# First loads of a linear attention kernel: three of four fp32 loads on SP's queue become casting loads on GpSimd's

## The chip, the core and the metric

The kernel runs on one core of a Trainium2 chip. A core has a matrix engine (TensorE, PE in the profile, with its weight loads as PEld), a vector engine (VectorE, DVE), a scalar engine (ScalarE, ACT), a general engine (GpSimd, POOL) and an engine that mostly issues transfers (SyncE, SP). The five run by themselves and meet at semaphores. Transfers between main memory (HBM) and the on-chip memory are issued by an engine and carried out by 16 DMA engines that all queues share. The metric is the device time of one execution in microseconds; 126.58 us is the median of three runs before the change (126.56 to 126.68).

## The reference

Linear attention with a ReLU feature map, over 96 heads (8 x 12), a sequence of 512 and a head size of 64, all in fp32:

```
Q_feat = np.maximum(0, Q)
K_feat = np.maximum(0, K)
KV = np.einsum('bhkd,bhkv->bhdv', K_feat, V)
K_sum = np.sum(K_feat, axis=2)
numerator = np.einsum('bhqd,bhdv->bhqv', Q_feat, KV)
denominator = np.einsum('bhqd,bhd->bhq', Q_feat, K_sum)
out = numerator / (denominator[:, :, :, None] + 1e-10)
```

Each of Q, K, V and the output is 12.58 MB. So 37.75 MB are read and 12.58 MB written, and each byte moves once.

## The kernel before

**Tiles.** The heads are cut into 24 groups of four for K and V, and into 12 steps of eight for Q and the output; a step `o` needs the groups `2o` and `2o + 1`. K or V of a group is one transfer that reads 0.5 MB in fp32, Q of a step one that reads 1 MB, the output of a step one store of 1 MB. Each lies as 128 rows (partitions), 4 KB of fp32 per row for K and V, 8 KB for Q and the output.

**Loads.** They are all written ahead of the compute. K and V of groups 0 and 1 come by SP (lines 103 to 107): four plain fp32 loads into two tiles `kv_first`, which take turns in the pool of the output tiles. Everything else comes by GpSimd (lines 92 to 100), in loads that cast to bf16 on the way, so that they write half of what they read: first Q of step 0 (line 108), then for each later step K and V of both groups and Q (lines 110 to 113). Behind the first Q, GpSimd makes the identity matrix (line 109, in two instructions). K tiles and V tiles have rings of 12 buffers, Q tiles 7. GpSimd's program is this list and nothing else.

**Compute.** For a group, `prep` (lines 136 and 138) makes on VectorE two masked ReLU copies of K (`kf`) and a masked copy of V (`vo`), and `prep_v` the other copy of V on ScalarE or VectorE (lines 143, 145). `mm_kv` (line 150) multiplies them into K-transposed times V, with the key sums beside it; `evac_kv` (line 160) copies that out of the accumulator. For a step, `qt` transposes Q on TensorE against the identity (line 171) and applies the ReLU (lines 177, 179); `denom` (lines 221 to 233) gives the reciprocal of the denominator; `out_t` (lines 201, 203) the numerator, transposed; `backs` transposes it back (line 239), multiplies by the reciprocal (line 245) and calls `store`. The last two steps are written out in finer pieces, with `out_u` in place of `out_t` for the last (lines 214, 216), and a few matmuls without a use (`idle`, line 188).

**Order.** The order of every engine's instructions is the order of the program text; semaphores are set from the data. Before the loop stand the preparation of groups 0 and 1, an fp32 copy of the identity by VectorE (line 270), the zeroing of buffers, the products of groups 0 and 1 and the transposes of Q of step 0.

**Stores.** A store by SP is held back. `store(o)` first issues a read of a few bytes from the K tile of the step that is five further on, into `scratch` (line 253), so that SP waits until that load has landed:

```
if o + DELAY < NO:
    nc.sync.dma_start(out=scratch, in_=k_sb[2 * (o + DELAY)][0:1, 0, :])
```

The first seven stores are held so; the rest follow as soon as they are computed (lines 258 and 260), and the last is issued in two halves.

Of the kernel before, what the change touches and what calls it, by code (L numbers as in the profile page):

```python
# [10 lines left out]
def kernel(  # L11
# [7 lines left out]
    nc = tc.nc  # L19
    B, H, S, D = Q.shape  # L20
    assert D == 64
    P = 128
# [4 lines left out]
    R = S * 4 // P  # L27
# [4 lines left out]
    NO = NG // 2  # L32
    assert NO * 8 == NH and R == 16 and RQ == 32
    DELAY = 5
    F32 = 2

    fp32 = mybir.dt.float32
    bf16 = mybir.dt.bfloat16
# [3 lines left out]
    def pool(name, bufs, **kw):  # L42
        return ctx.enter_context(tc.tile_pool(name=name, bufs=bufs, **kw))
# [7 lines left out]
    outp = pool("outp", DELAY + 2)  # L51
# [6 lines left out]
    def view(X, f):  # L58
        return X.rearrange("b h s d -> (b h s d)").rearrange("(n p f) -> n p f", p=P, f=f)

    Qr, Kr, Vr, Or = view(Q, RQ * D), view(K, R * D), view(V, R * D), view(out, RQ * D)
# [27 lines left out]

    q_sb, k_sb, v_sb = {}, {}, {}  # L90

    def load_kv(g):
        k_sb[g] = kin.tile([P, R, D], bf16, name="k_sb")
        nc.gpsimd.dma_start(out=k_sb[g].rearrange("p r d -> p (r d)"), in_=Kr[g], single_packet=True)  # L94
        v_sb[g] = vin.tile([P, R, D], bf16, name="v_sb")
        nc.gpsimd.dma_start(out=v_sb[g].rearrange("p r d -> p (r d)"), in_=Vr[g], single_packet=True)  # L96

    def load_q(o):
        q_sb[o] = qin.tile([P, U, 2 * D], bf16, name="q_sb")
        nc.gpsimd.dma_start(out=q_sb[o].rearrange("p u f -> p (u f)"), in_=Qr[o], single_packet=True)  # L100


    for g in range(F32):
        kv = outp.tile([P, 2, R, D], fp32, name="kv_first", tag="o_sb")
        k_sb[g], v_sb[g] = kv[:, 0], kv[:, 1]
        nc.sync.dma_start(out=k_sb[g].rearrange("p r d -> p (r d)"), in_=Kr[g])
        nc.sync.dma_start(out=v_sb[g].rearrange("p r d -> p (r d)"), in_=Vr[g])
    load_q(0)
    make_identity(nc, ident)
    for o in range(1, NO):  # L110
        load_kv(2 * o)
        load_kv(2 * o + 1)
        load_q(o)

    def zero(i):
# [146 lines left out]
    def out_tile():  # L262
        return outp.tile([P, RQ, D], fp32, name="o_sb", tag="o_sb")
# [50 lines left out]
    o = NO - 2  # L314
    g = 2 * NO - 2
# [9 lines left out]
    o_sb = out_tile()  # L325
# [42 lines left out]
```

## Time and profile before

| | |
|---|---|
| median of three runs | 126.58 us |
| the profiled execution | 126.52 us |
| its span, first to last instruction | 124.7 us |
| mean granted clock of TensorE | 0.95 |
| busy: PE, DVE, ACT, POOL | 86.0, 81.1, 79.3, 33.1 us |
| moved per second over the span, reads and writes of HBM | 403 GB/s |
| loads by SP before: K0, V0, K1, V1 | 4 of 512 KB written each |
| loads by GpSimd: K and V | 22 + 22 of 256 KB written each |
| loads by GpSimd: Q | 12 of 512 KB written each |

The profile is of one execution. Its times are in microseconds from the first instruction. A line of the timeline has a start, a duration, an engine, a line of the kernel and what was written from what; the bracket at its end is the idle time before it and what ended that. `SPq` is SP's issuing of a transfer, and L106 is line 106. Bandwidth in slices and windows is of bytes written, so a casting load shows half of what it reads. K0 stands for K of group 0, V1 for V of group 1, Q0 for Q of step 0, and so on.

### The profile page before, as it was taken

The page shows a single profiled execution, that of the slowest core. Times are in us where ns is not written, and L with a number is a line of the kernel's source. Part 1 is how long each engine was busy: PE and PEld are TensorE (multiplying, and loading weights), DVE is VectorE, ACT ScalarE, POOL GpSimd, SP SyncE. Part 2 cuts the span into 40 slices and gives each one's busy share as a digit, 9 for nine tenths or more (in the row PEclk, how much of TensorE's full clock was granted, in tenths as well). Part 3 has the DMA queues.
Part 4 walks back from the last instruction along what each step waited for, and adds up shares of the span by engine and source line. Part 5 has one row for each costly group of instructions (what it writes and reads, how often), then busy time and mean ns, then how long its engine had stood idle before and what let it go on. Part 6 is the DMA issues. An engine that isn't in the chain of part 4 may idle for free.

```text
span 124.7 us, 2672 instructions
## 1 busy us (share of the span) xinstructions
PE 86.0 (69%) x1075; PEld 78.5 (63%) x1075; DVE 81.1 (65%) x176; ACT 79.3 (64%) x114; POOL 33.1 (27%) x62
## 2 busy tenths in 40 slices
PE   0041196998989899894598599399777587797600
PEld 0040194997878788793597499299576486696500
DVE  2605743949798897979247845935928918979600
ACT  0251549989898997989249558666839646837100
POOL 6924433415253341142133124034022000000000
PEclk9999999999999999999769959958999999999996
DMA  3999999999999999999999999999999999999993
GB/s 133 322 285 277 216 205 210 213 210 215 207 213 208 210 214 327 257 215 300 282 215 282 302 213 258 324 213 234 342 223 218 322 257 215 319 416 420 426 416 143
DMA packets 10748, 32.68 MB, mean 262 GB/s; under 512 B 1392, under 2 KB 1392, under 8 KB 9328
## 3 DMA queue, kind: packets, MB, share of 16 engines
q0 software_dynamic: 8064, 17.83, 74.7%
q1 hardware_dynamic: 2672, 14.68, 29.2%
q8 instruction: 8, 0.13, 0.4%
q14 instruction: 4, 0.03, 0.1%
HBM read 37.75 MB, written 12.58 MB: 403 GB/s over the span
## 4 chain that ended last, share of the span: by engine, by line
DMA 34%; DVE 26%; PE 25%; ACT 5%; issue 2%; SPq 1%; DVEq 1%; ACTq 0%; POOLq 0%
DMA v_sb<-in_V_dram 14%; DVE o_sb L245 13%; DMA q_sb<-in_Q_dram 13%; PE ps_kv L150 11%; DMA kv_first<-in_V_dram 8%; PE ps_bk L239 6%; PE ps_qt L171 4%; DVE kf L136 3%; ACT qt L179 3%; DVE vo L138 3%; ACT kvd L160 2%; PE ps_ot L201 2%; DVE vo L145 2%; DVE den L229 1%; DVE rec L233 1%
## 5 line engine op out<-in xcount | busy, mean ns | idle before, releaser
L150 PE MATMUL ps_kv<-vo,kf 128*128 128x132 bf16 x384 | 31.3, 247 | 18.4 <-ACT vo L143 7.9
L150 PEld LDWEIGHTS <-kf 128*128 128x128 bf16 x384 | 28.9, 111 | 19.7 <-DVE vo L138 10.3
L245 DVE TENSOR_TENSOR o_sb<-ps_bk,rec 128x1024 f32<-128x1024 f32 x24 | 28.4, 1220 | 16.7 <-PE ps_bk L239 16.7
L160 ACT CAST kvd<-ps_kv 64x260 bf16<-64x260 f32 (+1 forms) x54 | 18.7, 346 | 19.0 <-PE ps_kv L150 16.8
L179 ACT ACTIVATE qt<-ps_qt 128x1024 bf16<-128x1024 bf16 x23 | 22.4, 1027 | 4.9 <-PE ps_qt L171 4.8
L203 ACT COPY ot_sb<-ps_ot 128x1024 f32<-128x1024 f32 x22 | 21.9, 1014 | 2.1 <-PE ps_ot L201 1.3
L239 PE MATMUL ps_bk<-ident,ot_sb 128*128 128x128 f32 x192 | 23.0, 273 | 0.0
L136 DVE TENSOR_SCALAR kf<-k_sb,mask 128x1024 bf16<-128x1024 bf16 x44 | 18.3, 457 | 5.8 <-DMA k_sb<-in_K_dram 5.8
L94 POOL DMA_DIRECT2D k_sb<-in_K_dram x22 | 12.7, 578 | 34.1 <-DMA q_sb<-in_Q_dram 16.8
L239 PEld LDWEIGHTS ps_bk<-ident,ot_sb 128*128 128x128 f32 x192 | 20.8, 141 | 0.0
L171 PE MATMUL ps_qt<-ident,q_sb 128*128 128x128 bf16 x192 | 15.3, 243 | 5.6 <-DMA q_sb<-in_Q_dram 5.6
L96 POOL DMA_DIRECT2D v_sb<-in_V_dram x22 | 13.1, 597 | 19.7 <-DMA k_sb<-in_K_dram 12.0
L171 PEld LDWEIGHTS <-q_sb 128*128 128x128 bf16 x192 | 13.7, 110 | 6.6 <-DMA q_sb<-in_Q_dram 6.4
L201 PE MATMUL ps_ot<-qt,kvd 128*128 128x256 bf16 x88 | 13.5, 284 | 4.0 <-DVE o_sb L245 4.0
L201 PEld LDWEIGHTS <-kvd 128*128 128x128 bf16 x88 | 8.5, 101 | 6.5 <-issue 5.4
L138 DVE TENSOR_SCALAR vo<-v_sb,mask 128x1024 bf16<-128x1024 bf16 x22 | 10.8, 489 | 1.6 <-DMA v_sb<-in_V_dram 1.6
L143 ACT ACTIVATE vo<-v_sb,mask 128x1024 bf16<-128x1024 bf16 x10 | 11.5, 1154 | 0.2
L221 PEld LDWEIGHTS <-qt 128*128 128x128 bf16 x192 | 6.7, 97 | 4.7 <-ACT qt L179 3.4
L221 PE MATMUL ps_den<-kvd,qt 128*128 128x16 bf16 x192 | 7.5, 179 | 2.6 <-ACT qt L179 2.1
L100 POOL DMA_DIRECT2D q_sb<-in_Q_dram x12 | 6.7, 558 | 8.0 <-DMA v_sb<-in_V_dram 5.0
L224 DVE SCALAR_TENSOR_TENSOR own<-ps_den,mask_h 128x256 f32<-128x256 f32 x12 | 5.0, 417 | 3.3 <-PE ps_den L221 3.3
L145 DVE TENSOR_SCALAR vo<-v_sb,mask 128x1024 bf16<-128x1024 bf16 x12 | 5.8, 484 | 0.0
(27 smaller groups left out, 29.5 us busy)
## 6 DMA issues: line engine op xcount, KB each, us to landing
out_dram<-o_sb SPq DMA_DIRECT2D x11, 1024.0 KB, 9.1
q_sb<-in_Q_dram POOLq DMA_DIRECT2D x12, 512.0 KB, 14.9
k_sb<-in_K_dram POOLq DMA_DIRECT2D x22, 256.0 KB, 13.9
v_sb<-in_V_dram POOLq DMA_DIRECT2D x22, 256.0 KB, 13.2
kv_first<-in_K_dram SPq DMA_DIRECT2D x2, 512.0 KB, 5.6
kv_first<-in_V_dram SPq DMA_DIRECT2D x2, 512.0 KB, 7.0
out_dram<-o_sb SPq DMA_DIRECT2D x2, 512.0 KB, 4.9
scratch<-k_sb SPq DMA_DIRECT2D x7, 0.1 KB, 4.8
```

Of the source, the lines that this page charges most:

```text
L96: nc.gpsimd.dma_start(out=v_sb[g].rearrange("p r d -> p (r d)"), in_=Vr[g], single_packet=True)
L136: nc.vector.tensor_scalar(kf[g][:, :, s, :], k_sb[g], scalar1=0.0, scalar2=mask[:, 0, s:s + 1], op0=Alu.max, op1=Alu.mult)
L138: nc.vector.tensor_scalar(vo[g % NB][:, :, 0, 2:D + 2], v_sb[g], scalar1=mask[:, 1, 0:1], scalar2=None, op0=Alu.mult)
L150: nc.tensor.matmul(ps_kv[:, g % 2, 0:2 * (D + 2)].rearrange("p (t d) -> p t d", t=2), kf[g][:, r, :, :].rearrange("p s d -> p (s d)"), vo[ ...
L160: copy(kvd[o % NK][64 * c:64 * c + 64, 4 * gs.start + s:4 * gs.stop:2, c * D1:c * D1 + D1].rearrange("p (g t) d -> p g t d", t=2), ps_kv[6 ...
L171: nc.tensor.transpose(ps[:, u, :], q_sb[o][:, i * (U // 2) + u, :], ident)
L179: nc.scalar.activation(to, ps, Act.Relu)
L201: nc.tensor.matmul(ps[:, i], kvd[o % NK][:, h, 1:2 * D + 1], q[:, :, h, :], start=True, stop=True, skip_group_check=True)
L203: nc.scalar.copy(ot[o][:, :, 4 * j:4 * j + 4], ps.rearrange("p h u c -> p u h c"))
L221: nc.tensor.matmul(ps[:, u], qt_sb[o % NZ][:, u, :], kvd[o % NK][:, :, 0:2 * D1:2 * D1 - 1], start=True, stop=True, skip_group_check=True)
L239: nc.tensor.transpose(ps[:, 2 * v:2 * v + 2].rearrange("p c d -> p (c d)"), ot[o][:, 8 * j + v].rearrange("p h c -> p (h c)"), ident32)
L245: nc.vector.tensor_tensor(o_sb[:, rs], ps, rec[o][:, rs].unsqueeze(2).to_broadcast([P, 16, D]), op=Alu.mult)
```

## The change

Only K0 is still loaded by SP in fp32. V0, K1 and V1 become casting loads of GpSimd's queue, in bf16 tiles of the usual rings, ahead of Q0 in the program; all further loads follow in their old order. The function that loaded K and V together is split in two. The `kv_first` pool tile keeps its shape and half of it is used; there is one such tile instead of two.

```
-    def load_kv(g):
+    def load_k(g):
         k_sb[g] = kin.tile([P, R, D], bf16, name="k_sb")
         nc.gpsimd.dma_start(out=k_sb[g].rearrange("p r d -> p (r d)"), in_=Kr[g], single_packet=True)
+
+    def load_v(g):
         v_sb[g] = vin.tile([P, R, D], bf16, name="v_sb")
         nc.gpsimd.dma_start(out=v_sb[g].rearrange("p r d -> p (r d)"), in_=Vr[g], single_packet=True)
...
-    for g in range(F32):
-        kv = outp.tile([P, 2, R, D], fp32, name="kv_first", tag="o_sb")
-        k_sb[g], v_sb[g] = kv[:, 0], kv[:, 1]
-        nc.sync.dma_start(out=k_sb[g].rearrange("p r d -> p (r d)"), in_=Kr[g])
-        nc.sync.dma_start(out=v_sb[g].rearrange("p r d -> p (r d)"), in_=Vr[g])
+    k_sb[0] = outp.tile([P, 2, R, D], fp32, name="kv_first", tag="o_sb")[:, 0]
+    nc.sync.dma_start(out=k_sb[0].rearrange("p r d -> p (r d)"), in_=Kr[0])
+    load_v(0)
+    load_k(1)
+    load_v(1)
     load_q(0)
     make_identity(nc, ident)
     for o in range(1, NO):
-        load_kv(2 * o)
-        load_kv(2 * o + 1)
+        for g in (2 * o, 2 * o + 1):
+            load_k(g)
+            load_v(g)
         load_q(o)
```

More of the change, by code (lines that the diff above doesn't have):

```diff
@@ L34 @@
     DELAY = 5
-    F32 = 2
     fp32 = mybir.dt.float32
```

## The prediction

> **What bounds the kernel now.** I read the busy lines of the page first, then windows of the span, then the start in order of time, and last the DMA issues and the tail.
>
> The page's slices and totals (40 slices of 3.1 us; tenths of the 16 DMA engines busy, then bytes written per second):
>
> ```profile
> span 124.7 us, 2672 instructions
> DMA  3999999999999999999999999999999999999993
> q0 software_dynamic: 8064, 17.83, 74.7%
> q1 hardware_dynamic: 2672, 14.68, 29.2%
> HBM read 37.75 MB, written 12.58 MB: 403 GB/s over the span
> ```
>
> No compute engine is over 69% busy, while the DMA engines are full in every slice but the first and the last. GB/s counts bytes written: a casting load (q0, GpSimd's queue) reads two for each one it writes, so its figure is doubled below to compare with fp32 loads and stores (q1, SP's queue).
>
> Windows of the span (start:end, length, busy time of PE, PEld, DVE, ACT, POOL, granted clock, DMA share, GB/s written):
>
> ```profile
> 2.00:2.50 0.50, 0.00 (x0) 0.00 (x0) 0.17 (x2) 0.00 (x0) 0.42 (x3) 1.00 0.69 262
> 2.50:3.00 0.50, 0.00 (x0) 0.00 (x0) 0.00 (x0) 0.00 (x0) 0.50 (x2) 1.00 1.07 418
> 3.00:4.50 1.50, 0.00 (x0) 0.00 (x0) 0.37 (x1) 0.00 (x0) 1.50 (x3) 1.00 1.01 404
> 4.50:4.75 0.25, 0.00 (x0) 0.00 (x0) 0.25 (x1) 0.00 (x0) 0.25 (x1) 1.00 1.18 377
> 4.75:5.00 0.25, 0.00 (x0) 0.00 (x0) 0.25 (x2) 0.00 (x0) 0.25 (x2) 1.00 1.03 213
> 5.00:12.00 7.00, 1.92 (x16) 1.75 (x16) 2.91 (x7) 2.44 (x2) 2.90 (x6) 1.00 1.06 278
> 12.00:25.00 13.00, 8.68 (x95) 7.90 (x96) 8.09 (x25) 9.63 (x16) 5.64 (x9) 1.00 1.10 211
> 110.00:122.00 12.00, 6.58 (x93) 5.96 (x91) 6.98 (x10) 3.59 (x5) 0.00 (x0) 1.00 1.00 420
> ```
>
> Casting loads alone (12 to 25 us) move 2 x 211 = 422 GB/s, stores alone (110 to 122) 420, SP's fp32 loads alone (3.0 to 4.5) 404. So the 50.3 MB (37.75 + 12.58) take about 120 us at any mix, and the time is: when the DMA engines start, plus the bytes, plus holes, plus the end. Where the rate halves (377 to 213, at about 4.75 us) the first casting packets, those of Q0, begin.
>
> The start in order of time (start, duration, engine, line, what):
>
> ```profile
> 0.74 0.38 SPq L106 DMA_DIRECT2D kv_first<-in_K_dram  x1
> 1.19 0.41 SPq L107 DMA_DIRECT2D kv_first<-in_V_dram  x1
> 1.24 0.66 POOL L100 DMA_DIRECT2D q_sb<-in_Q_dram  x1 [0.79 <-POOLq L352]
> 4.13 1.42 DVE L136 TENSOR_SCALAR kf<-kv_first,mask 128x1024 bf16<-128x1024 f32 x2 [1.74 <-DMA kv_first<-in_K_dram]
> 9.35 1.01 POOL L94 DMA_DIRECT2D k_sb<-in_K_dram  x1 [2.49 <-DMA q_sb<-in_Q_dram]
> 12.08 0.75 DVE L138 TENSOR_SCALAR vo<-kv_first,mask 128x1024 bf16<-128x1024 f32 x1 [1.18 <-DMA kv_first<-in_V_dram]
> 117.71 1.46 SPq L258 DMA_DIRECT2D out_dram<-o_sb  x2
> ```
>
> K0 is there at 4.13, V1 only at 12.08. POOL stops at its ninth load until the first has landed: eight are in flight. The chain of waits gives V's first loads 8% of the span; I don't read that as a gain, since the engines that deliver V1 are full. The last line is the last store, behind others still draining.
>
> How long a small transfer takes from issue to landing (the page's DMA issues, and the answer for line 106):
>
> ```profile
> scratch<-k_sb SPq DMA_DIRECT2D x7, 0.1 KB, 4.8
> DMA to landing us min/median/max: 3.4/5.6/7.8
> ```
>
> The 0.1 KB read of `scratch`, on SP's queue while GpSimd's is full, takes 4.8 us; K0 with 512 KB on idle engines takes 3.4, of which about 1.3 is data (0.524 MB at 404).
>
> **The change, part by part.** The profiled execution took 126.52 us, a span of 124.7 and 1.8 around it; the median is 126.58, 0.06 more, so I add 0.06 at the end.
>
> *Three loads leave SP's queue (V0, K1, V1), three casting loads come into GpSimd's.* HBM is read the same 37.75 MB. The rate differs. Written until 4.75: before 3.0, 131 + 209 = 340 KB; to 4.5, 606; to 4.75, 94; together 1,040 KB. In 4.75 to 5 another 53. That leaves 2,097 - 1,093 = 1,004 KB of SP's loads for 5 to 12, where 7 x 278 = 1,946 KB are written; so casts wrote 942 and read 1,884, and the stretch moved 2,888 KB. From 3 to 12 us that is 606 + 147 + 2,888 = 3,641 KB in 9.0 us, 405 GB/s. At the 422 of casting loads alone it takes 8.63 us, 0.37 less. K0 stays fp32, and about a microsecond of mixing stays with it: I take -0.3. Ends: 0, if the 405 belongs to the start and not to the queue, and -0.37.
>
> *When does GpSimd's first load reach the engines?* Today SP's four loads keep them full until casts join. Afterwards SP gives only K0: 340 KB by 3.0 and the other 184 at 404, done at about 3.5 us. V0 is now POOL's first instruction, at 1.24. Its first packet on idle engines is shown nowhere. From below: SP's first came about 1.1 us after its issue (0.74 to about 1.8, by the zoomed slices of the first 3 us), which puts V0 at 2.3 and makes no hole. From above: Q0's came 3.5 us after the same issue time, at 4.75, a hole of 4.75 - 3.5 = 1.25. I take the lower end, for two reasons. Q0's packets begin when K0 and V0 are through: 1,040 KB by 4.75, against their 1,049. A lag of GpSimd's own would not meet that border. And a queue that joins full engines waits: the scratch read takes 4.8 us with nothing to carry, against 3.4 - 1.3 = 2.1 for K0, so 2.7 us are work already taken in. Less that, Q0's 3.5 becomes about 1, so the 1.1 of SP's is near. Cost taken: 0; ends 0 and +1.25. The Trainium skill (DMA: Bandwidth & Descriptors, section Latency and other measured facts) has a first byte after about 1 us by GpSimd and 0.6 by SP; by its difference an estimate is 2.3 + 0.4 = 2.7 us, no hole, the same sum; no trace here shows it.
>
> *POOL's instructions.* V0, K1, V1 stand ahead: at 0.55 us each, with 0.66 for a first, Q0 is issued at about 2.9 instead of 1.24, the identity (0.5 us) is made at 3.5 to 4.1 instead of 1.9 to 2.5, and every later load is issued 1.7 us later, until eight are in flight. Cover: one K or V load is 1.25 us of DMA work and 0.55 of issue, so the queue stays fed; V0 to Q0 alone (2.6 MB) last until 9.7 us. The identity's first reader, DVE's cast, runs at 12.7; it may move up to about 9, still behind. Without the cover, 1.7 us.
>
> *Landings.* In one queue's order at 422: V0 is through at 4.75, K1 6.0, V1 7.2, Q0 9.7, and about 0.7 on top to be seen. V0 is as today (5.4), V1 4 us earlier, Q0 1.4 later (9.0 to 10.4), and the first transposes, which today start at 16.9, can start at about 11. V0 and V1 cost DVE 0.49 instead of 0.75, K1's two passes 0.46 each instead of 0.75: 1.1 us less of DVE. All of this ends in no time saved: stores wait for the loads of five steps on (`scratch`), and these for bytes. Priced at 0, hidden by full DMA engines; with them idle the 4 us would count.
>
> *SP, buffers, end.* SP issues three loads fewer (1.3 us) and then has nothing until 42.8: 0. K1, V0 and V1 now take buffers in the 12-deep rings, so K13 waits for K1's reader, V12 and V13 for those of V0 and V1, done some 30 us before: 0. At the end 110 to 122 is pure stores; at 117.71 about 5 us of draining remain and the last store is 2.5 of them (1.05 MB at 420), so compute has some 1.3 us to spare after its issue's 1.1. It moves with the last load and stays covered.
>
> Sum: 126.52 - 0.3 + 0 + 0 = 126.22, with the 0.06, **126.3 us**.
>
> **Rivals.** *A hole behind K0 (slower).* Place: 3.5 to 4.75 us, all 16 engines idle. Price: 1.25, less the 0.3: 126.58 + 0.95 = 127.5. It decides once V0's first packet is later than 3.5 + 0.3 = 3.8 us, and shows as slower from 4.05. For it: Q0's packets do start 3.5 us after issue, in the only case that is there. If engines take turns between queues, Q0 would have begun as soon as its descriptors were there, so 4.75 would be their true time. Against: the border at K0 + V0 and the 4.8 us of `scratch`. The Trainium skill (same page, section Queues, rings and completion order) says engines go round the queues packet by packet, which is that turn-taking; the 4.8 us for 0.1 KB agree with it only if much is taken in before a turn.
>
> *Hidden anyway.* The 405 of the start is the price of starting, or of HBM at that moment, not of the queue. For it: the page's slices of casting loads alone vary by themselves, 205 to 216 GB/s written. Time 126.6, within 126.4 to 126.7.
>
> *Earlier compute counts.* If the early order of work and not the bytes set the end, V1's 4 us would come off in part: down to 122.6. Against: full slices throughout.
>
> **How the numbers follow.** A run of this kernel tells about 0.2% (0.25 us) from no change. Forecast (gain of 0.1 to 0.4, 126.2 to 126.5): 0.55. Hidden anyway: 0.17. Hole: 0.26, with all values of it from a small one up to 127.5. Earlier compute: 0.02. About three quarters of the forecast pass 126.33, so faster is 0.41 + 0.02 = 0.43; same is 0.14 from the forecast, 0.13 from hidden and 0.01 from a small hole, 0.28; slower is 0.25 of hole and 0.04 of hidden, 0.29. The range goes from 126.0 (the -0.37 and a little for the ramp before 3 us) to 127.5; the forecast's own is 126.1 to 126.5.
>
> **What would show it.** Right: DMA share about 1 in each half microsecond from 2.5 us on, written GB/s near 211 from about 4 us, V1's first reader on DVE at about 8, the first transposes near 11, the last load and the last store each about 0.3 earlier. Wrong: a window between 3.5 and 5 us with a share well under 1 (the hole), or 420 in the first 12 us with an end that has not moved (the end is compute's).

## The result and the profile after

The changed kernel takes 128.68 us (median of five runs, 127.98 to 128.91) against 126.58 for the kernel before beside it. The two medians are 2.1 us apart; the ratio taken over all these runs is 1.0146, with a 95% interval of 1.0117 to 1.0175: it is 1.5% slower. The profiled execution took 128.70 us. Medians and ratios, here and below, are of fast runs; a single run (129.06 us, with Q0 first) was a slow one and is left out.

The page after, totals and the slices of the DMA engines:

```profile
span 126.9 us, 2674 instructions
DMA  4999999999999999999999999999999999999991
GB/s 141 138 204 205 211 212 209 216 207 213 210 212 211 206 218 302 277 216 262 316 215 249 335 212 225 353 213 212 345 237 214 323 257 217 357 422 421 408 396 53
q0 software_dynamic: 8496, 18.62, 77.6%
q1 hardware_dynamic: 2240, 13.11, 25.6%
HBM read 37.75 MB, written 12.58 MB: 397 GB/s over the span
```

The same bytes are read and written, and 0.8 MB of what is written on the chip has gone (three loads write half). The row of busy tenths still says full everywhere. The row of GB/s does not: the second slice (3.2 to 6.3 us) has 138, where casting loads alone run at 204 to 216.

Windows of the changed kernel (columns as in the prediction; the last two are DMA share and GB/s written):

```profile
2.50:3.00 0.50, 0.00 (x0) 0.00 (x0) 0.00 (x0) 0.00 (x0) 0.50 (x2) 1.00 1.02 385
3.00:3.50 0.50, 0.00 (x0) 0.00 (x0) 0.00 (x0) 0.00 (x0) 0.50 (x2) 1.00 1.34 315
3.50:4.00 0.50, 0.00 (x0) 0.00 (x0) 0.00 (x0) 0.00 (x0) 0.42 (x2) 1.00 0.56 70
4.00:4.50 0.50, 0.00 (x0) 0.00 (x0) 0.34 (x1) 0.00 (x0) 0.50 (x2) 1.00 0.67 123
4.50:5.00 0.50, 0.00 (x0) 0.00 (x0) 0.50 (x2) 0.00 (x0) 0.50 (x1) 1.00 2.05 160
5.00:5.50 0.50, 0.00 (x0) 0.00 (x0) 0.50 (x1) 0.00 (x0) 0.50 (x2) 1.00 0.56 94
5.50:6.00 0.50, 0.00 (x0) 0.00 (x0) 0.08 (x1) 0.00 (x0) 0.50 (x2) 1.00 0.71 131
6.00:7.00 1.00, 0.00 (x0) 0.00 (x0) 0.00 (x0) 0.00 (x0) 0.76 (x2) 1.00 1.00 174
12.00:25.00 13.00, 10.76 (x114) 9.71 (x112) 6.36 (x20) 9.48 (x17) 4.76 (x9) 1.00 1.10 211
```

K0 alone fills the time from 2.5 to 3.3 us, and the casting load V0 begins right behind it (first packet at 3.31). Then the engines deliver 70 to 174 instead of 211 for three and a half microseconds. Against 211 the five half microseconds from 3.5 to 6 lack 141, 88, 51, 117 and 80 GB/s, and the full one from 6 to 7 lacks 37: 275 KB written, 551 KB read, 1.3 us at 422 as a mean over the 16 engines. From 12 us on the rate is what it was. A share over 1 (2.05) with a low rate means packets that last long: in the packet records of the trace, seven casting packets begun between 3.9 and 5.0 us took 1.5 to 1.95 us, where 0.17 is usual.

The changed kernel in order of time, the lines that answer to those shown of before:

```profile
0.74 0.39 SPq L105 DMA_DIRECT2D kv_first<-in_K_dram  x1
1.24 0.66 POOL L97 DMA_DIRECT2D v_sb<-in_V_dram  x1 [0.79 <-POOLq L354]
4.02 1.02 POOL L93 DMA_DIRECT2D k_sb<-in_K_dram  x1
4.17 1.42 DVE L138 TENSOR_SCALAR kf<-kv_first,mask 128x1024 bf16<-128x1024 f32 x2 [1.77 <-DMA kv_first<-in_K_dram]
7.66 0.49 DVE L140 TENSOR_SCALAR vo<-v_sb,mask 128x1024 bf16<-128x1024 bf16 x1 [2.07 <-DMA v_sb<-in_V_dram]
10.15 0.49 DVE L140 TENSOR_SCALAR vo<-v_sb,mask 128x1024 bf16<-128x1024 bf16 x1 [0.37 <-DMA v_sb<-in_V_dram]
15.02 1.91 PE L173 MATMUL ps_qt<-ident,q_sb 128*128 128x128 bf16 x16
119.89 1.46 SPq L260 DMA_DIRECT2D out_dram<-o_sb  x2
```

V0 is there at 7.66 (5.4 before), V1 at 10.15 (12.08 before), the first transposes start at 15.0 (17.0 before). So the early compute is two microseconds ahead, and the last store is issued 2.2 us later, 119.89 against 117.71: the end follows the loads and not the early compute. The end of the span, first two lines before the change, then two after:

```profile
122.00:123.00 1.00, 0.00 (x0) 0.00 (x0) 0.00 (x0) 0.00 (x0) 0.00 (x0) 0.70 0.61 242
123.00:124.00 1.00, 0.00 (x0) 0.00 (x0) 0.00 (x0) 0.00 (x0) 0.00 (x0) 0.50 0.13 53
```

```profile
123.00:124.00 1.00, 0.00 (x0) 0.00 (x0) 0.00 (x0) 0.00 (x0) 0.00 (x0) 0.50 0.79 315
124.00:126.00 2.00, 0.00 (x0) 0.00 (x0) 0.00 (x0) 0.00 (x0) 0.00 (x0) 0.50 0.16 61
```

The mean loss of 1.3 us is less than the 2.2 of the end. The trace keeps 16 landing marks for each load, as many as there are engines, and they show the difference. Of V0's marks eleven come between 5.14 and 5.74 us and five only between 6.97 and 7.63: the stall takes some engines and not others. This unevenness stays: the marks of V3 lie between 15.68 and 17.63, before between 15.08 and 15.58. With V3 both kernels have read the same loads. Its first mark is 0.6 us later than before, the mean of the 16 is 1.2 later, the last 2.05, and a load is usable only with its last mark. So the end follows the engines that stood still longest. This is a reading of the traces, which no run was made to test; but over the profiled executions of all 14 kernels of this study the span goes with V3's last mark (correlation 0.93) more closely than with the mean of its marks (0.85).

### The profile page after: what moved, and what is told of

It is laid out like the page before. It is cut to its first block, busy times and chain, and to the rows that moved or that the text cites. A ratio compares the mean times of both kernels' runs of the same rounds, so it can differ in the third digit from the quotient of the medians.

```text
span 126.9 us, 2674 instructions
## 1 busy us (share of the span) xinstructions
PE 87.6 (69%) x1075; PEld 79.0 (62%) x1075; DVE 80.3 (63%) x176; ACT 79.6 (63%) x114; POOL 33.4 (26%) x65
## 3 DMA queue, kind: packets, MB, share of 16 engines
q0 software_dynamic: 8496, 18.62, 77.6%
## 4 chain that ended last, share of the span: by engine, by line
DMA 60%; PE 17%; DVE 15%; issue 2%; DVEq 1%; POOL 1%; ACT 0%; POOLq 0%
DMA q_sb<-in_Q_dram 26%; DMA v_sb<-in_V_dram 19%; DMA k_sb<-in_K_dram 15%; DVE o_sb L247 7%; PE ps_kv L152 7%; PE ps_bk L241 5%; PE ps_qt L173 4%; DVE kf L138 2%; DVE vo L140 1%; DVE vo L147 1%; DVEq L365 1%; DVE den L231 1%; DVE rec L235 1%; DVE qt L179 1%; DVE own L226 1%
## 5 line engine op out<-in xcount | busy, mean ns | idle before, releaser
L152 PE MATMUL ps_kv<-vo,kf 128*128 128x132 bf16 x384 | 30.6, 245 | 15.6 <-ACT vo L145 10.2
L152 PEld LDWEIGHTS <-kf 128*128 128x128 bf16 x384 | 28.4, 110 | 16.6 <-DVE vo L140 9.1
L138 DVE TENSOR_SCALAR kf<-k_sb,mask 128x1024 bf16<-128x1024 bf16 x46 | 19.2, 461 | 8.7 <-DMA k_sb<-in_K_dram 8.6
L173 PE MATMUL ps_qt<-ident,q_sb 128*128 128x128 bf16 x192 | 16.7, 256 | 9.1 <-DMA q_sb<-in_Q_dram 9.0
L93 POOL DMA_DIRECT2D k_sb<-in_K_dram x23 | 13.4, 583 | 35.5 <-DMA q_sb<-in_Q_dram 19.1
L173 PEld LDWEIGHTS <-q_sb 128*128 128x128 bf16 x192 | 14.4, 117 | 11.6 <-DMA q_sb<-in_Q_dram 11.3
L140 DVE TENSOR_SCALAR vo<-v_sb,mask 128x1024 bf16<-128x1024 bf16 x24 | 11.6, 485 | 4.8 <-DMA v_sb<-in_V_dram 4.8
L145 ACT ACTIVATE vo<-v_sb,mask 128x1024 bf16<-128x1024 bf16 x12 | 13.8, 1153 | 0.2
```

The lines of the kernel that those rows point to most:

```text
L138: nc.vector.tensor_scalar(kf[g][:, :, s, :], k_sb[g], scalar1=0.0, scalar2=mask[:, 0, s:s + 1], op0=Alu.max, op1=Alu.mult)
L145: nc.scalar.activation(vo[g % NB][:, :, 1, 2:D + 2], v_sb[g], Act.Copy, scale=mask[:, 1, 1:2])
L152: nc.tensor.matmul(ps_kv[:, g % 2, 0:2 * (D + 2)].rearrange("p (t d) -> p t d", t=2), kf[g][:, r, :, :].rearrange("p s d -> p (s d)"), vo[ ...
L173: nc.tensor.transpose(ps[:, u, :], q_sb[o][:, i * (U // 2) + u, :], ident)
```

## The experiments

My first theories for the stall were three. A: VectorE's two passes over K0, which run from 4.17 us, keep GpSimd from writing descriptors (the lists that DMA engines work off). B: the identity matrix that GpSimd makes between its loads delays them. C: GpSimd's first loads start slowly by themselves, and SP's three other loads had covered that. Each ratio below is against the kernel before, run beside the variant; the changed kernel was not run again beside them, so ratios are to be compared with its 1.0146.

**VectorE later.** VectorE's first instruction on data waits for V1, so that its passes over K0 come behind the stall (`prep` is split for it into `prep_k` and `prep_v0`):

```
     for g in range(2):
         zero(g)
-        prep(g)
-        prep_v(g, nc.scalar)
+    prep_v0(1)
+    for g in range(2):
+        prep_k(g)
+        if g == 0:
+            prep_v0(g)
+        prep_v(g, nc.scalar)
```

> The changed kernel, but VectorE's first instruction on loaded data is the one on V1, so that its two passes over K0 (4.17 to 5.59 us in the changed kernel) come after V0, K1 and V1 have landed. Same loads, same queues. Theory A (VectorE's passes over K0 hold GpSimd off the descriptors of the loads in flight, and the DMA engines stand still for it): no window between 3.5 and 7 us with a written rate under 180 GB/s, V1 landed near 7.9 us, 126.2 to 126.8 us. Theory B (the identity matrix that GpSimd makes between its loads is what delays them): unchanged, 128.0 to 128.9 us. Theory C (GpSimd's first loads start slowly by themselves, and only SP's loads covered it): unchanged, 128.0 to 128.9 us, with 90 to 130 GB/s at 5.0 to 6.0 us.

Measured: 128.08 us (127.58 to 128.53), ratio 1.0123 [1.0093, 1.0153]. The trace has VectorE idle, and GpSimd's issue takes its usual time, yet the engines stand still:

```profile
4.02 0.56 POOL L93 DMA_DIRECT2D k_sb<-in_K_dram  x1
5.00:5.50 0.50, 0.00 (x0) 0.00 (x0) 0.00 (x0) 0.00 (x0) 0.50 (x2) 1.00 0.69 106
```

A falls as the main cause. (The issue at 4.02 took 1.02 us in the changed kernel beside VectorE, 0.56 here, so VectorE does slow GpSimd's issue. That the ratio is a little under the changed kernel's is within the noise of both; a few tenths of a microsecond by VectorE aren't excluded.)

**Identity later.**

```
     load_q(0)
-    make_identity(nc, ident)
     for o in range(1, NO):
         ...
         load_q(o)
+        if o == 1:
+            make_identity(nc, ident)
```

> The changed kernel with the identity matrix made after the loads of step 1 have been issued instead of right behind Q0. Theory A: the stall stays, 128.0 to 128.9 us. Theory B: the stall is gone, 126.2 to 126.9 us. Theory C: 128.0 to 128.9 us.

Measured: 128.12 us, ratio 1.0122 [1.0101, 1.0142], with 74 GB/s at 5.0 to 5.5 us. B falls.

**More work on VectorE.**

```
+    dumb = consts.tile([P, 2, 1024], fp32, name="dumb")
     for g in range(2):
         zero(g)
+        if g == 0:
+            nc.vector.memset(dumb[:, 0], 0.0)
+            for _ in range(4):
+                nc.vector.tensor_copy(dumb[:, 1], dumb[:, 0])
         prep(g)
```

> The changed kernel with work added on VectorE alone, ahead of its passes over K0: one zeroing of 128x1024 fp32 and four fp32 copies of 128x1024 within the on-chip memory, some 3 us from 2.4 us on, of no use to the result. The passes over K0 then run at about 5.5 to 7 us. Theory A: the descriptors are held off from 2.4 us on, the stall grows by 1 to 3 us: 129.3 to 131.5 us. Theories B and C: nothing on the path is touched, 128.0 to 128.9 us.

Measured: 128.16 us, ratio 1.0136 [1.0103, 1.017]: no slower than the changed kernel. Three microseconds of fp32 copies from 3.6 us on added nothing, which is a second no to A (forecast by it: 129.3 to 131.5).

**Half the change.** V0 goes back to SP; K1 and V1 stay casting loads.

```
     ...
+    k_sb[0], v_sb[0] = kv[:, 0], kv[:, 1]
     nc.sync.dma_start(out=k_sb[0].rearrange("p r d -> p (r d)"), in_=Kr[0])
-    load_v(0)
+    nc.sync.dma_start(out=v_sb[0].rearrange("p r d -> p (r d)"), in_=Vr[0])
     load_k(1)
     load_v(1)
```

> Half of the change: K0 and V0 by SP in fp32, K1 and V1 as casting loads in front of Q0. SP's loads keep the DMA engines full until about 4.8 us instead of 3.5. Theory A: VectorE's passes over K0 and V0 still run from 4.2 to 6.2 us, when the casting packets have just begun; a stall remains but is shorter, 0.3 to 1.4 us: 126.6 to 127.9 us. Theory B: the identity is made at about 2.9 to 3.6 us, behind Q0's issue, while SP still feeds: 126.3 to 126.8. Theory C, with a slow start that lasts until a fixed time after the first issue (about 6.5 us): 127.2 to 128.0 us.

Measured: 127.02 us (126.64 to 127.33), ratio 1.0027 [1.0009, 1.0045], and no stall at the start. The time lies in A's wide range and below C's; but A's stall is not there, although VectorE's passes over K0 run from 4.21 to 5.75 us beside the first casting packets, and C's range was for a slow time that ends at a fixed moment. The window 5 to 7 us, here and then in the changed kernel:

```profile
5.00:7.00 2.00, 0.00 (x0) 0.10 (x1) 1.61 (x5) 1.53 (x2) 1.68 (x4) 1.00 1.11 209
```

```profile
5.00:7.00 2.00, 0.00 (x0) 0.00 (x0) 0.58 (x1) 0.00 (x0) 1.75 (x4) 1.00 0.82 143
```

K1 was issued at 1.24 us, as V0 is in the changed kernel; the engines reached it at 4.67 instead of 3.31, and it ran at full rate. What is left of 0.27% is not explained. It does not come from the start: V3's last mark is at 15.34 us, 0.24 earlier than before. That trace has a dip of its own at 45 to 47 us (174 and 144 GB/s, where the kernel before has 225 and 215).

Of the first theories C was left, in three forms: C1, a casting load is not ready for some 3.5 us after its issue; C2, casting loads are slow until a fixed time, whichever they are; C3, the packet form of these loads does it.

**Without single packets.** The first four casting loads are issued with `single_packet=False`.

> The changed kernel, but the first four casting loads (V0, K1, V1, Q0) are issued without the option that makes one packet of each engine's share of a load. Theory C3 (an engine starts on its share only when the whole packet is there, and that makes the stall): stall much smaller, 126.4 to 127.4 us. Theories C1 and C2: no difference, 127.9 to 128.9 us.

Measured: 128.39 us, ratio 1.0152 [1.0118, 1.0187], as C1 and C2 have it. C3 falls as far as this option tests it: number and sizes of the packet records are the same in both traces (8496 on GpSimd's queue), so that no record shows the option to have changed the packets.

**Q0 first.** GpSimd's order is Q0, V0, K1, V1.

> The changed kernel with Q0 issued first on GpSimd's queue, then V0, K1 and V1; K0 by SP as before. Q0 carries twice the bytes per row, so the queue has 2.5 us of work in its first load instead of 1.25. Theory C1 (a casting load that the engines reach within some 3.5 us of its issue is not ready on all engines; the stall goes by a load's age): Q0 is reached at age 2.2 us and may stall, V0 is reached at 5.9 us with an age of 4 and does not; the stall is halved or gone, 126.4 to 127.5 us. Theory C2 (casting loads are slow until a fixed time, about 6.5 us, whichever they are): as in the changed kernel, 127.9 to 128.9 us, with a written rate under 130 GB/s between 5.0 and 5.5 us.

Measured: 127.42 us (127.12 to 128.58), ratio 1.0065 [1.004, 1.0091]. Less of a loss, and the median is in C1's range; but the profiled execution, at 128.58, is in C2's, and in it the stall was there, on Q0 itself (131 to 180 GB/s between 3.5 and 6.5 us). The run does not decide between C1 and C2.

**Half the change, GpSimd 0.6 us later.** The identity and one zeroing of 128x640 stand in front of GpSimd's loads:

```
+    pause = consts.tile([P, 640], bf16, name="pause")
+    make_identity(nc, ident)
+    nc.gpsimd.memset(pause, 0.0)
     load_k(1)
     load_v(1)
     load_q(0)
-    make_identity(nc, ident)
```

> K0 and V0 by SP in fp32, as in the half change that showed no stall, but GpSimd first makes the identity and a further zeroing of its own, so that its first casting load (K1) is issued at about 2.5 us instead of 1.24 and is reached at 4.75 us with an age of 2.2, as V0 is in the changed kernel. Theory C1: the stall is back, 1.3 us later than in the changed kernel (windows under 150 GB/s written between 5.5 and 7.5 us), 127.8 to 129.0 us. Theory C2: little or none, since the casts begin when the slow time is nearly over, 126.8 to 127.4 us.

Measured: 127.41 us, ratio 1.008 [1.0056, 1.0104]; the time lies between the two forecasts. The delay came out at 0.6 us and not 1.3 (K1 was issued at 1.82). That was enough to bring a stall back into the half change, ahead of the 5.5 to 7.5 us that C1 named:

```profile
5.00:6.00 1.00, 0.00 (x0) 0.00 (x0) 1.00 (x3) 0.25 (x1) 1.00 (x3) 1.00 0.61 125
6.00:7.00 1.00, 0.00 (x0) 0.10 (x1) 0.65 (x3) 1.00 (x1) 0.57 (x1) 1.00 1.11 205
```

**No load by SP.** K0 too comes by GpSimd, in front.

> No load by SP at all: K0 too is a casting load of GpSimd's queue, in front of V0, K1, V1 and Q0. It shows the first packet and the stalls of the software queue with nothing beside it. Theory C1: first packets at about 3.3 us, then stalls within K0 and V0 of the changed kernel's size or more (1.5 to 2 us); with the 1.5 us without SP's K0 together 2.5 to 3.5 us over the kernel before: 129.0 to 130.5 us. Theory C2: first packets at about 3.3 us and slow until about 6.5 us, then full: the same sum within half a microsecond, 129.0 to 130.0 us. A first packet before 2.6 us would speak against both.

Measured: 128.39 us, ratio 1.0143 [1.0112, 1.0175], as slow as the change although nothing moves before 2.6 us, and faster than either theory had it. This run changed my mind. The windows, for GpSimd's K0 (issued at 1.24), V0 (1.90) and K1 (2.41):

```profile
2.00:2.50 0.50, 0.00 (x0) 0.00 (x0) 0.17 (x2) 0.00 (x0) 0.50 (x2) 1.00 0.00 0
2.50:3.00 0.50, 0.00 (x0) 0.00 (x0) 0.00 (x0) 0.00 (x0) 0.50 (x2) 1.00 0.59 70
3.00:5.50 2.50, 0.00 (x0) 0.00 (x0) 0.64 (x2) 0.00 (x0) 2.42 (x6) 1.00 1.12 202
5.50:6.00 0.50, 0.00 (x0) 0.00 (x0) 0.24 (x1) 0.00 (x0) 0.50 (x2) 1.00 0.97 94
6.00:6.50 0.50, 0.00 (x0) 0.00 (x0) 0.37 (x1) 0.32 (x1) 0.50 (x2) 1.00 1.04 127
```

On idle engines the first casting load starts 1.4 us after its issue, and two run at full rate, the second at an age of 2 us: C1 as I had put it falls, and C2 is hard to keep with a full rate from 3.0 to 5.5 us. The third, issued about when the first data began to move, stands still on some engines at an age of 3 us; its last long packets end at about 7.2, 4.8 us after its issue. Hence theory D: a load issued on idle engines runs after about 1.4 us; one issued while they are busy needs 3.5 to 5 us until all of them run it, and only work already queued covers that. "Busy" is a close call here: what the loads that stood still up to here share is an issue that was not over when the first data moved (V0 of the changed kernel: issue 1.24 to 1.90, first data at 1.76; K1 here: 2.41 to 2.96, first data at 2.60), while V0 here was issued by 2.44.

**The kernel before, GpSimd's loads late.** The identity and four zeroings stand in front of Q0:

```
+    pause = consts.tile([P, 640], bf16, name="pause")
+    make_identity(nc, ident)
+    for _ in range(4):
+        nc.gpsimd.memset(pause, 0.0)
     load_q(0)
-    make_identity(nc, ident)
```

> The kernel before the change, with its four loads by SP, but GpSimd makes the identity and zeroes an unused tile four times before its first load, so that Q0 is issued at about 4.2 us instead of 1.24. SP's loads alone last until about 7.1 us. Theory D: Q0 is reached at an age of about 3 us and is not ready on all engines before 8 to 9 us; a stall between 7 and 9 us with windows under 150 GB/s written, 127.4 to 128.8 us. Theory C2: by then the slow time is over; no stall, and less mixing of the two queues, 126.2 to 126.8 us.

Measured: 127.71 us (126.56 to 128.07), ratio 1.0075 [1.005, 1.0101]. C2 falls: with SP's four loads untouched and Q0 issued at 3.89, four of Q0's packets took 1.0 to 1.1 us (0.32 is usual) and ended at about 9.0, far behind the supposed slow time. The windows show less than I forecast behind 7 us (no half microsecond under 180, where D had under 150), and something that I had not forecast at all ahead of it, where SP's loads alone run:

```profile
4.50:5.50 1.00, 0.00 (x0) 0.00 (x0) 1.00 (x3) 0.16 (x1) 1.00 (x2) 1.00 0.85 311
8.50:9.00 0.50, 0.50 (x7) 0.50 (x5) 0.50 (x2) 0.00 (x1) 0.50 (x2) 1.00 0.87 180
```

**No load by SP, Q0 first.** GpSimd's order is Q0, K0, V0, K1, V1.

> No load by SP, and GpSimd's order is Q0, K0, V0, K1, V1. In the run without SP's loads the first two loads (K0 and V0, 2.5 us of work together) ran at full rate from 2.6 us on and the third stood still on some engines from 5.4 to 7.2 us. Here Q0 alone is 2.5 us of work, so that the third load (V0) is reached at about 6.4 us instead of 5.2, at an age of 4 us. Theory D: first packets at about 2.6 us, the stall smaller by about 1 us or gone; 127.0 to 127.8 us. Theory C2: the same stall at 5 to 7 us, 127.8 to 128.6 us.

Measured: 127.75 us, very steady (127.69 to 127.81), ratio 1.0099 [1.0085, 1.0113]. The stall of the third load is gone, as D has it: 205 GB/s from 5.5 to 8.0 us. A hole that no theory had is there instead, at the first packets; eight of them, begun at 2.6 us, took 0.9 to 1.2:

```profile
3.00:3.50 0.50, 0.00 (x0) 0.00 (x0) 0.00 (x0) 0.00 (x0) 0.50 (x2) 1.00 0.33 57
3.50:5.50 2.00, 0.00 (x0) 0.00 (x0) 0.00 (x0) 0.00 (x0) 1.93 (x5) 1.00 1.03 207
5.50:8.00 2.50, 0.00 (x0) 0.00 (x0) 0.40 (x1) 0.00 (x0) 1.35 (x4) 1.00 1.09 205
```

**K0 held back.** Same loads and queues as the change, but SP's K0 is issued at 2.56 us, behind V0 and K1:

```
-    nc.sync.dma_start(out=k_sb[0].rearrange("p r d -> p (r d)"), in_=Kr[0])
     load_v(0)
     load_k(1)
+    nc.gpsimd.memset(k_sb[0][:, 0, 0:1], 0.0)
+    nc.sync.dma_start(out=k_sb[0].rearrange("p r d -> p (r d)"), in_=Kr[0])
```

> The changed kernel, same loads in the same queues, but SP's K0 is held until GpSimd has issued V0 and K1 (GpSimd writes one column of K0's tile behind them, which the load overwrites), so that K0 is issued at about 2.6 us instead of 0.74 and V0 and K1 meet idle engines. Theory D (a load issued on idle engines runs after some 1.4 us, one issued on busy engines needs 3.5 to 5): the first data moves at about 2.6 us, 0.8 later than in the changed kernel, V0 and K1 run at full rate to 5.1 us or later (windows from 3.0 to 5.0 us near 200 GB/s written, where the changed kernel has 70 to 160), V1 and Q0 may stand still a little as in the run without SP's loads; 127.3 to 128.4 us in all. If instead the casting loads stand still whenever they are among the first that run, with SP's load before or behind them: the stall comes on top of the later start, 129.0 to 130.0 us.

Measured: 128.18 us, ratio 1.0127 [1.0105, 1.0148]. The plainest sign for D: V0 and K1, on idle engines, now run through, and it is SP's K0 that comes late (first packet at 5.40, 2.8 us after its issue, where 1.0 is enough in the changed kernel; 6.8 us from issue to landing, 3.4 there).

```profile
3.00:5.00 2.00, 0.00 (x0) 0.00 (x0) 0.00 (x0) 0.00 (x0) 1.93 (x5) 1.00 1.06 192
kv_first<-in_K_dram SPq DMA_DIRECT2D x1, 512.0 KB, 6.8
```

The changed kernel has 167 in the window of the first line and 143 in the two microseconds after. The time is hardly better: data begins to move 0.8 us later, which eats most of what the missing stall gives back.

**A third of the change.** K0, V0 and K1 by SP; only V1 is a casting load in front of Q0.

> K0, V0 and K1 by SP in fp32; only V1 is a casting load, in front of Q0 (the last third of the change alone). SP's loads last until about 6.0 us. Theory D (a casting load that is issued while the DMA engines are busy takes some 4 to 5 us from its issue until all engines run it, and SP's loads are the work that covers this; one issued on idle engines takes 1.4): V1, issued at 1.24, is reached at 6.0 and ready on all engines: no stall, no window from 2.5 to 12 us with a written rate under 190 GB/s; 126.3 to 126.7 us. Theory C2 (casting loads are slow until some 6.5 us, whichever they are): no stall either, the same time; this run tells whether the whole loss goes when the cover is long enough.

Measured: 126.59 us against 126.60, ratio 1.0004 [0.9996, 1.0013]. No stall, no loss, and no gain either.

No kernel of the study beat the one before.

## Why the prediction was wrong

The forecast was 126.3 us, slightly faster, in 126.0 to 127.5; measured were 128.68, slower and outside that range. By its steps:

**The bound held.** The DMA engines set the time, the bytes stayed, compute two microseconds ahead in the first stage saved nothing. The rival of earlier compute was rightly given little.

**The step that failed is "When does GpSimd's first load reach the engines? ... Cost taken: 0".** The start itself was right: V0's packets begin at 3.3 us, right behind K0, with no gap of 1.25 us on all engines. On idle engines GpSimd's queue starts 1.4 us after issue (2.6 us, the run without SP's loads), near the 1.1 taken from SP. The Trainium skill's 1 us against 0.6 (DMA: Bandwidth & Descriptors, Latency and other measured facts) had given 2.7 as an estimate by its difference; the trace agrees with it, though both latencies by themselves are longer here, 1.4 and 1.0 to 1.1.

What I missed is that a load that has begun is not yet a load that runs on all 16 engines: five of V0's 16 shares landed 1.2 us and more behind the other eleven. The term put at 0 measured 1.3 us of lost transfer in the mean of the engines and 2.05 us on the slowest, with the end 2.2 later. I had a row that hinted at it: 4.8 us for a 0.1 KB read on busy engines. I read it as waiting behind other work, subtracted 2.7 us from Q0's 3.5, and then used only the remainder.

For the first packet that reading held: in the four runs with two to four loads by SP and GpSimd's first issue at 1.24 or 1.82, its first packet came at 4.65 to 4.73 us, behind K0 and V0. By D the time does not vanish when those loads go; it is a time that work already queued must cover. SP's K0 is 1.3 us of such work; the four loads of before were over 5. The runs give the border: with two loads by SP (2.6 us of work at 404 GB/s) and GpSimd's first issue at 1.24 us there was no stall, with the same two and the issue 0.6 us later there was one. Counted from the end of GpSimd's issue to the first packet: with 2.75 to 2.8 us in between (the kernel before, the half and the third of the change) the load ran at once on all engines; with 1.4 (the change), 2.2 (the half with GpSimd late) and 2.4 (the kernel before with GpSimd late) it stood still on some.

**The cover named for POOL's instructions was the wrong quantity.** "One K or V load is 1.25 us of DMA work and 0.55 of issue, so the queue stays fed" compares issue times. The queue was fed, with issues at 1.24, 1.90, 2.42 and 2.94 us; what was fed did not yet run on all engines.

**The rival of the hole had the sign and the place, but not the mechanism, and too small a price.** It ran from 3.5 us and was priced at 1.25 less 0.3; measured are 2.1 us. It was to be decided by a first packet of V0 later than 3.8 us, and that came at 3.31. It is no clean hole of all engines but 3.5 us in which some stand still, 1.3 us in the mean. Its sign in the windows, a share well under 1 (0.56 at 3.5 us), did come.

**The gain of 0.3 us did not reach the end.** The 405 GB/s of the first 12 us were put down to SP's fp32 loads. (That sum leaves out 29 KB written before 2.0 us; with them it is 408, and the most to be gained 0.30 instead of 0.37.) With one load moved and no stall the ratio is 1.0004 [0.9996, 1.0013]; a third of 0.3 us would be 0.9992, just outside that interval. The half change, two loads moved and no stall at the start, should have been at 0.9984 and is at 1.0027, although V3's last mark came 0.24 us earlier in it than before. With one load moved that mark came 0.03 later. So a small gain at the start is possible, but nothing shows it in the time, and the rival of no gain was the nearer one on this term.

**Landings.** V0 was forecast as before (5.4) and came at 7.66, V1 at about 7.9 and came at 10.15, the first transposes at 11 and came at 15.0: all late by the stall. The last store moved by +2.2 us instead of -0.3.

## What to carry to other kernels

Where the DMA engines are the bound, ask of the first loads how much queued work stands behind each queue's start: in the runs with a stall the last of the long packets ended 4 to 5.7 us after the stalled load's issue, and 2.6 us of plain loads, issued earlier in the other queue, hid it. A row for a tiny transfer under load (4.8 us for 0.1 KB) is a warning of such a latency; plan a cover for it instead of subtracting it. And the busy tenths of DMA engines can read 9 while some of them stand still inside packets, as in the second slice of the changed kernel (138 GB/s instead of 204 to 216): look at the bytes.

## What the runs showed of the hardware that I had not expected

The stall is uneven and varies: the changed kernel spreads over 0.9 us in five runs (127.98 to 128.91), the kernel before over 0.3 (126.55 to 126.83), and the variant whose hole left the engines level (no load by SP, Q0 first: Q0's 16 landing marks within 0.3 us) over 0.1 in four.

The Trainium skill (SBUF — State Buffer, Who interferes with whom) says that VectorE in its modes with two ports keeps GpSimd from writing descriptors, so that such loads starve. The trace agrees for the issue: 1.02 us beside VectorE's passes, 0.56 without them. It does not carry the loss here: taking the passes away left 128.08 us, and adding 3 us of fp32 copies 128.16.

The DMA: Bandwidth & Descriptors page of the Trainium skill, section Queues, rings and completion order, lets each DMA engine go round its queues packet by packet. Under strict turns K0, issued at 2.56 us behind two casting loads, should have had its first turn soon after. Its first packet came 2.8 us after its issue, so a queue's first turn on busy engines comes late here, for SP's queue as for GpSimd's.

What remains open is where on the way from the issue to the engines these microseconds pass, and why only some of the engines wait. Nor is it explained why a load reached too early stands until 4 to 5.7 us after the start of its issue, when one reached at 3.4 us runs at once. Open too are two observations that D does not explain: SP's own loads fell to 311 GB/s between 4.5 and 5.5 us when GpSimd issued its first load at 3.89 (the kernel before with GpSimd late), some 0.3 us of that run's loss of 1.1 by an estimate at 404 GB/s, and Q0 as the very first load made a hole of about a microsecond at its first packets, where K0 in its place made none.
